# Chained down products, ScalarE evictions and VectorE products in a Hymba encoder layer

## The chip, the core and the metric

The kernel runs on one core of a Trainium2 chip. TensorE multiplies matrices into PSUM; VectorE, ScalarE and GpSimd (DVE, ACT and POOL in the rows) work element by element, the first two from PSUM or SBUF, and SyncE (SP) issues the DMAs. Each engine runs its own instructions strictly in its program order and waits at semaphores for the others. The metric is the device time of one execution in microseconds.

## What is computed

One bidirectional encoder layer for 1024 positions of width 1024, in float32. Cut to what matters here:

```python
h = modulate(rms_norm(x, attn_norm_w), sh_a, sc_a)
q_g, k_g, v_g, r_g, lr_f, lr_b, q_d, k_d, v_d = split_columns(h @ w_in, IN_SIZES)
o_a = gla_chunked(q, k, v, decay_fwd) + flipped gla_chunked(..., decay_bwd)   # 4 heads, chunks of 64
o_a = rms_norm(o_a, gla_norm_w) * silu(r_g)
a   = softmax(q1 k1 + bias) - lam * softmax(q2 k2 + bias)                    # 4 heads, blocks of 128 queries
o_b = rms_norm(a @ v_d, diff_norm_w) * (1 - lambda_init)
x   = x + g_a * (concat(o_a, o_b) @ w_out)
h2  = modulate(rms_norm(x, ffn_norm_w), sh_f, sc_f)
gate, val = split(depthwise_conv3(h2 @ w_up, conv_w, conv_b))
x   = x + g_f * ((silu(gate) * val) @ w_down)                                # 2816 x 1024
out = rms_norm(x, final_norm_w)
```

## The kernel before

Every large product is made of three matmuls: an operand is split into a high part (a cast to fp32r on ScalarE, line 370) and the rest (a subtraction, line 371), and `mm3` adds high by high, high by low and low by high (lines 565 to 567). Up and down projections go by a Strassen scheme, seven products of half size in place of eight.

The stages in order of time: the first projections (to about 350 us); attention in 32 steps of one head and 128 queries each, with GLA worked in between in the first 16 steps and the output projection (`gen_wout`) in the last 16; the transition (second norm, transposes, the operands of up); the up products; the down products; the rest of the last outputs. A framework orders each engine's instructions from a simulated timeline, so the order of instructions on an engine isn't that of the code.

**Attention.** `att_probs` makes scores (line 842), adds the bias and takes the maximum on VectorE (845) and the exponential on ScalarE (850); twice, for the two maps. `att_mix` combines them (858, 860). `att_T` transposes the result into two PSUM tiles of four blocks and copies the first to `aT` by ScalarE (871), the second by VectorE (873). `att_out` multiplies with v (888), scales into `on` (889) and, once for four query blocks, normalises: squares, Ln and Exp on ScalarE (895 to 897), the product `on` by rstd on GpSimd (898).

**GLA.** Per head `gd`, the queries times a decay, is made on GpSimd (1022); `kn` is a ScalarE copy of transposed keys (1029) for the state matmuls (1034). The output of each half is normalised (1088 to 1098), multiplied by the gate on GpSimd (1099), and split: `ohi` on ScalarE, the low part `go` on GpSimd.

**Output projection.** The list `wo` in `KN` says how many pieces of it each of the last 16 attention steps takes in.

**Down.** Seven products p1, p7, p6, p5, p4, p3, p2, each with 11 units of 128 rows of w_down, 4 blocks t of 128 positions and 3 matmuls: 132 matmuls of 128x512. A step is a pair of units; `down_load` loads blocks of weights (da) and of the gated activations (db) three steps ahead, `down_prep` makes sums and splits one step ahead: `dp_hi` and `whi_dp` on ScalarE, `db_p` and `wlo_dp` on VectorE. Products at even places write four one-bank tiles (tags mm and ao), those at odd places two tiles of two banks each (tag S); the pools have two tiles of each tag, which is all of PSUM. `down_out` takes a block of a product out of PSUM as soon as its last matmul is in, and adds it to the running sums; p5 and p4 gate their sums with g_f, add them to the residual x1b and multiply by the final norm's weight, all on GpSimd (lines 1538, 1539, 1565, 1571); p3 and p2 do the last of it on VectorE and ScalarE, and end each block of 128 positions with a norm (1580 to 1585) and its output DMA.

## Time and profile before

| | us |
|---|---|
| median of 3 runs | 1389.1 |
| lowest and highest | 1386.96, 1390.07 |
| the profiled execution | 1388.06 |
| its span, first to last instruction | 1386.4 |
| TensorE busy in the span | 1302.7 |
| VectorE, ScalarE, GpSimd busy | 978.6, 634.5, 389.0 |
| mean granted clock of TensorE, of 2.4 GHz | 0.974 |

Read it from the stage downwards: windows tell how busy each engine is in a stretch and what clock TensorE had; waits tell what ended the idle time of an engine; the timeline lists single instructions with their start and length. Busy time of matmuls overlaps a little, since one is 0.39 us long and the next starts 0.227 us later.

### The profile page before, as it was taken

The numbers are of one execution on the slowest core, as the hardware profiler recorded it, in microseconds if no ns is written. First come the engines' busy times: TensorE is split into PE (matmuls) and PEld (weight loads), VectorE is DVE, ScalarE is ACT, GpSimd is POOL, SyncE is SP. The second block draws the span as 40 slices with busy tenths as digits, with TensorE's granted clock in tenths as the row PEclk, the third lists the DMA queues.
The fourth block names the chain that finished last, engine by engine and source line by source line (L and its number), as shares of the span: only waits on it lengthen the run. The fifth ranks groups of instructions, "written<-read, shape, count | busy, mean of one in ns | idle before, by whom it ended". The sixth has DMA issues, their size and how long they took to land.

```text
span 1386.4 us, 17727 instructions
## 1 busy us (share of the span) xinstructions
PE 1302.7 (94%) x6244; PEld 1069.5 (77%) x6244; DVE 978.6 (71%) x1433; ACT 634.5 (46%) x1058; POOL 389.0 (28%) x284
## 2 busy tenths in 40 slices
...
GB/s 275 216 70 229 175 215 226 297 330 359 343 230 206 210 217 256 284 259 221 207 61 68 130 98 106 100 96 119 129 129 122 114 170 149 388 254 178 143 47 122
DMA packets 197873, 261.57 MB, mean 189 GB/s; under 512 B 13914, under 2 KB 122711, under 8 KB 197783
## 3 DMA queue, kind: packets, MB, share of 16 engines
...
## 4 chain that ended last, share of the span: by engine, by line
PE 69%; DVE 12%; DMA 5%; issue 4%; ACT 3%; POOL 3%; SPq 2%; ACTq 0%; DVEq 0%; POOLq 0%
PE st_up_b L565 4%; PE st_up_b L566 4%; PE st_up_b L567 4%; PE s L842 3%; PE dp L566 3%; PE dp L565 3%; PE dp L567 3%; PE o L888 3%; PE st_up_c L566 3%; PE st_up_c L567 3%; PE st_up_c L565 3%; PE st_up_a L566 2%; PE st_up_a L565 2%; PE st_up_a L567 2%; PE wo_ps L567 2%
## 5 line engine op out<-in xcount | busy, mean ns | idle before, releaser
L371 POOL TENSOR_TENSOR wlo_up<-raw_up,whi_up 128x512 fp32r<-128x512 f32 x132 | 176.3, 1342 | 211.7 <-ACT whi_up L370 203.5
L370 ACT CAST whi_up<-raw_up 128x512 fp32r<-128x512 f32 x132 | 80.8, 618 | 110.9 <-PE st_up_b L566 61.1
L566 PE MATMUL dp<-wlo_dp,dp_hi 128*128 128x512 f32 x308 | 121.1, 393 | 8.3 <-DVE wlo_dp L371 8.3
L565 PE MATMUL dp<-whi_dp,dp_hi 128*128 128x512 f32 x308 | 119.9, 391 | 2.8 <-DVE dacc L1562 2.8
L567 PE MATMUL dp<-whi_dp,db_p 128*128 128x512 f32 x308 | 119.0, 391 | 0.0
L566 PE MATMUL st_up_b<-t_lo,whi_up 128*128 128x512 f32 x264 | 103.4, 392 | 4.4 <-DVE t_lo L394 4.4
L565 PE MATMUL st_up_b<-t_hi,whi_up 128*128 128x512 f32 x264 | 103.6, 393 | 3.8 <-ACT t_hi L390 2.7
L567 PE MATMUL st_up_b<-t_hi,wlo_up 128*128 128x512 f32 x264 | 102.8, 390 | 0.0
L850 ACT ACTIVATE p<-p,mx 128x1024 f32<-128x1024 f32 x64 | 73.5, 1149 | 50.1 <-DVE mx L845 49.8
L845 DVE CUSTOM_DVE_ANT_0 p<-s,bias 128x1024 f32<-128x1024 f32 x64 | 77.3, 1217 | 14.9 <-PE s L842 12.9
L1432 ACT ACTIVATE cv<-u,cw 128x1024 f32<-128x1024 f32 x44 | 53.2, 1210 | 61.0 <-DVE u L433 61.0
L842 PE MATMUL s<-k,q 128*128 128x512 f32 x256 | 78.0, 427 | 2.4 <-DMA k<-k_d 1.5
L566 PEld LDWEIGHTS dp<-wlo_dp,dp_hi 128*128 128x128 f32 x308 | 58.1, 189 | 22.4 <-DVE wlo_dp L371 10.4
L371 DVE TENSOR_TENSOR wlo_dp<-da_p,whi_dp 128x512 fp32r<-128x512 f32 x77 | 67.8, 896 | 8.1 <-ACT whi_dp L370 7.9
L888 PEld LDWEIGHTS o<-vd,aT 128*128 128x128 f32 x512 | 66.7, 199 | 6.8 <-issue 1.7
L371 DVE TENSOR_TENSOR db_p<-db_p,dp_hi 128x1024 fp32r<-128x1024 f32 (+1 forms) x42 | 59.6, 1425 | 16.9 <-ACT dp_hi L370 16.9
L565 PE MATMUL st_up_a<-b_hi,whi_up 128*128 128x512 f32 x176 | 68.9, 392 | 2.3 <-DVE b L384 1.3
L565 PEld LDWEIGHTS dp<-whi_dp,dp_hi 128*128 128x128 f32 x308 | 58.2, 189 | 15.3 <-DVE dacc L1562 3.2
L888 PE MATMUL o<-vd,aT 128*128 128x128 f32 x512 | 68.8, 284 | 0.9 <-ACT aT L871 0.9
L370 ACT CAST whi_dp<-da_p 128x512 fp32r<-128x512 f32 x77 | 46.4, 620 | 49.5 <-PE dp L567 37.5
L566 PE MATMUL st_up_a<-b_lo,whi_up 128*128 128x512 f32 x176 | 68.5, 389 | 0.0
L567 PEld LDWEIGHTS dp<-whi_dp,db_p 128*128 128x128 f32 x308 | 58.3, 189 | 12.1
...
## 6 DMA issues: line engine op xcount, KB each, us to landing
...
```

What stands on the lines that cost most here:

```text
L370: S.copy(out=dst_hi, in_=src)
L371: lo_eng.tensor_tensor(out=dst_lo, in0=src, in1=dst_hi.bitcast(F32), op=ALU.subtract)
L565: T.matmul(ps, wh, rh, start=first, stop=False, skip_group_check=more)
L566: T.matmul(ps, wh, rl, start=False, stop=False, skip_group_check=more)
L567: T.matmul(ps, wl, rh, start=False, stop=last, skip_group_check=more)
L842: T.matmul(s[:, tsl(n)], q4[:, 2 * m + sw, :], kd[h][m][:, tsl(n)], start=(sw == 0), stop=(sw == 1))
L845: V.tensor_tensor_reduce(out=t, in0=s, in1=bias, scale=1.0, scalar=3.0e38, op0=ALU.add, op1=ALU.min, accum_out=mx)
L850: S.activation(t, t, AF.Exp, scale=-1.0, bias=mx, accum_out=z[:, m:m + 1])
L888: T.matmul(o_ps, aT[:, k, :], vd[h // 2][k // 4][:, k % 4, psl(h % 2)], start=(k == 0), stop=(k == KT - 1))
L1432: S.activation(t, u[b], AF.Identity, scale=cw[:, 44 + ci:45 + ci], bias=cw[:, 132 + ci:133 + ci])
```

## The change

Down's order becomes p1 p2 p6 p7 p5 p4 p3, and products that share outputs are accumulated on top of one another in PSUM: p2 on p1, p7 and then p4 on p6, p3 on p5. `down_out` so adds running sums less often: s1 is p1, s2 is p6 + p1 from PSUM, s3 is p7 (on p6) + p1, and p5 and p4 come on those. The block a12 is loaded twice, x1b's first half at the start of p2. The first four position blocks are finished in p4 (`finish`, with final weights), the others in p3.

In attention both halves of aT are copied by ScalarE; `gd`, the gate product with the low split behind it, and the product with rstd move from GpSimd to VectorE. The list `wo` is 2 2 and 3 3 where it was 1 1 and 2 4.

```diff
-  'wo': [3, 2, 2, 2, 2, 2, 1, 1, 2, 4, 3, 3, 3, 2, 3, 3], ... 'x01': (3, 4)
+  'wo': [3, 2, 2, 2, 2, 2, 2, 2, 2, 3, 3, 3, 3, 2, 3, 3], ... 'x01': (3, 3), ...
+  'dord': 'p1 p2 p6 p7 p5 p4 p3', 'aTs': '01', 'ons': 0, 'goe': 'VV', 'q3v': 1, 'onv': 1
...
-            if g == KN["aT"]:
+            if str(g) in KN["aTs"]:
                 S.copy(out=aT[:, 4 * g:4 * g + 4, :], in_=ps)
...
-        G.tensor_tensor(out=on, in0=on, in1=ss.unsqueeze(2).to_broadcast([P, 4, P]), op=ALU.mult)
+        if KN["onv"]:
+            V.tensor_tensor(out=on, in0=on, in1=ss.unsqueeze(2).to_broadcast([P, 4, P]), op=ALU.mult)
...
-        G.tensor_tensor(out=q3.rearrange("p (n c) -> p n c", c=CH), in0=q2.rearrange("p (n c) -> p n c", c=CH),
+        (V if KN["q3v"] else G).tensor_tensor(out=q3.rearrange("p (n c) -> p n c", c=CH), in0=q2.rearrange("p (n c) -> p n c", c=CH),
...
-            G.tensor_tensor(out=o, in0=o, in1=r_t[:, tsl(th)], op=ALU.mult)
+            eg[KN["goe"][0]].tensor_tensor(out=o, in0=o, in1=r_t[:, tsl(th)], op=ALU.mult)
...
-            split(hi, lo, o, G)
+            split(hi, lo, o, eg[KN["goe"][1]])
...
-    LOADS = {"p1": ("a11",), "p7": ("a21",), "p6": ("a22",), "p5": ("a21", "a22"), "p4": (), "p3": ("a12",), "p2": ()}
+    LOADS = {"p1": ("a11",), "p2": ("a12", "a21"), "p6": ("a22",), "p7": (), "p5": ("a21", "a22"), "p4": (), "p3": ("a12",)}
+    BANK = {"p1": ("A", True), "p2": ("A", False), "p6": ("B", True), "p7": ("B", False), "p4": ("B", False),
+            "p5": ("C", True), "p3": ("C", False)}
...
-            mm3(prods[p][t], bh[:, i, psl(t)], bl[:, i, psl(t)], *ws[i], u == 0, u == NU - 1)
+            mm3(ps_of[t], bh[:, i, psl(t)], bl[:, i, psl(t)], *ws[i], new and u == 0, u == NU - 1, not new)
...
+        elif p == "p2":
+            x1_add(t, 0, ps, half(f"dt_{p}{t}"), (V, G))
+            half_sq(t, 0)
+        elif p == "p6":
+            tmp = half(f"dt_{p}{t}", tag="sum")
+            V.tensor_tensor(out=tmp, in0=ps, in1=s1, op=ALU.add)
+            s2_of[t] = tmp
         elif p == "p7":
-            acc2[t] = half(f"dacc2_{t}")
-            S.copy(out=acc2[t], in_=ps)
+            V.tensor_tensor(out=kept(s3_of), in0=ps, in1=s1, op=ALU.add)
...
         elif p == "p5":
-            V.tensor_tensor(out=tmp, in0=ps, in1=acc2[t], op=ALU.add)
-            V.tensor_tensor(out=acc1[t], in0=ps, in1=acc1[t], op=ALU.add)
+            tmp = s3_of[t // 2][:, t % 2, :]
+            V.tensor_tensor(out=tmp, in0=ps, in1=tmp, op=ALU.add)
...
-            x1_add(4 + t, 0, acc1[t], acc1[t], (G, G))
+            x1_add(4 + t, 0, s2_of[t], s2_of[t], (G, G))
         elif p == "p4":
-            V.tensor_tensor(out=acc2[t], in0=ps, in1=acc2[t], op=ALU.add)
-            x1_add(t, 1, acc2[t], acc2[t], (G, G))
+            V.tensor_tensor(out=tmp, in0=ps, in1=s1, op=ALU.add)
+            x1_add(t, 1, tmp, tmp, (G, G))
             half_sq(t, 1)
-            G.tensor_tensor(out=x1[t][:, TH:], in0=x1[t][:, TH:], in1=fin_w[:, TH:], op=ALU.mult)
-            p1 = p1_of[t // 2][:, t % 2, :]
-            x1_add(t, 0, p1, p1, (G, G))
+            finish(t, False)
...
+        else:
+            V.scalar_tensor_tensor(out=o, in0=o, scalar=rs, in1=fin_w, op0=ALU.mult, op1=ALU.mult)
+            nc.sync.dma_start(out=out[0, psl(t), :], in_=o)
```

What this does to the order of instructions, at the places that the prediction speaks of. First ScalarE in the GLA half of attention, around the cast `ohi` of head 0 and the copy `kn2` of the keys of head 2, before:

```order
L850 ACTIVATE p1_3_1_4744,z_1_3_4711<-p1_3_1_4744,mx_1_3_1_4745 128x1024
L370 CAST ohi0_0_4558<-go0_0_4536 128x512
L1088 COPY go0_1_4638<-go0_1_4625 128x512
L850 ACTIVATE p2_0_0_4783,z_2_0_4786<-p2_0_0_4783,mx_2_0_0_4784 128x1024
L1090 ACTIVATE gsq0_1_4640<-go0_1_4638 128x512
L895 ACTIVATE osq_1_3_4886,oss_1_0_4591<-on1_0_4590 128x128
L1096 ACTIVATE gsq0_1_4640<-ms0_1_4642,eps_c_88 128x512
L1097 ACTIVATE gsq0_1_4640<-gsq0_1_4640 128x512
L370 CAST ohi0_1_4648<-go0_1_4638 128x512
L1029 COPY kn2_0_4793<-kn_ps2_0_4794 128x512
```
and after, from the same exponential on:

```order
L370 CAST ohi0_0_4558<-go0_0_4536 128x512
L1094 COPY go0_1_4638<-go0_1_4625 128x512
L1096 ACTIVATE gsq0_1_4640<-go0_1_4638 128x512
L871 COPY aT1_2_4753<-aT_ps1_2_0_4754 128x512
L871 COPY aT1_2_4753<-aT_ps1_2_1_4760 128x512
L850 ACTIVATE p1_3_1_4744,z_1_3_4711<-p1_3_1_4744,mx_1_3_1_4745 128x1024
L1102 ACTIVATE gsq0_1_4640<-ms0_1_4642,eps_c_88 128x512
L850 ACTIVATE p2_0_0_4783,z_2_0_4786<-p2_0_0_4783,mx_2_0_0_4784 128x1024
L1103 ACTIVATE gsq0_1_4640<-gsq0_1_4640 128x512
L898 ACTIVATE osq_1_3_4886,oss_1_0_4591<-on1_0_4590 128x128
L370 CAST ohi0_1_4648<-go0_1_4638 128x512
```
Between the two casts `ohi` the second copy of aT has come in; `kn2_0` follows the second `ohi` as before.

VectorE at the end of p5, whose evictions (`dt_p52`, `dacc1_2`) stand among splits for p4 and p3, before:

```order
L371 TENSOR_TENSOR wlo_dp4_3_0_12123<-da22_p5_3_11762,whi_dp4_3_0_12122 128x512
L1495 TENSOR_TENSOR da11_p1_2_10961<-da12_p3_2_12236,da11_p1_2_10961 128x1024
L371 TENSOR_TENSOR db_p3_0_12156<-db_p3_0_12156,dp3_hi0_12241 128x1024
L371 TENSOR_TENSOR wlo_dp4_3_1_12127<-da22_p5_3_11762,whi_dp4_3_1_12126 128x512
L1561 TENSOR_TENSOR dt_p52_12014<-dp5_1_11779,dacc2_2_11507 128x512
L1562 TENSOR_TENSOR dacc1_2_11751<-dp5_1_11779,dacc1_2_11751 128x512
L371 TENSOR_TENSOR wlo_dp4_4_0_12170<-da22_p5_4_11806,whi_dp4_4_0_12169 128x512
```
VectorE at the end of p6 after the change, where p6's sums (`dt_p60` and on) stand among splits for p7:

```order
L371 TENSOR_TENSOR wlo_dp7_1_1_11785<-da21_p2_1_11223,whi_dp7_1_1_11784 128x512
L1578 TENSOR_TENSOR dt_p60_11758<-dp6_0_11564,dp1_0_11279 128x512
L371 TENSOR_TENSOR db_p7_4_11812<-db_p7_4_11812,dp7_hi4_11900 128x1024
L371 TENSOR_TENSOR wlo_dp7_2_0_11818<-da21_p2_2_11260,whi_dp7_2_0_11817 128x512
L1578 TENSOR_TENSOR dt_p61_11763<-dp6_0_11564,dp1_0_11279 128x512
L1578 TENSOR_TENSOR dt_p62_11768<-dp6_1_11565,dp1_2_11288 128x512
L1578 TENSOR_TENSOR dt_p63_11773<-dp6_1_11565,dp1_2_11288 128x512
```
A split of 128x1024 and one of 128x512 lie between the first and the second eviction out of the tile `dp6_0`.

TensorE at the end of the first product in the tiles of two banks, p7 before:

```order
L567 MATMUL dp7_0_11296<-whi_dp7_5_0_11450,db_p7_5_11364 128x512
L565 MATMUL dp7_1_11297<-whi_dp7_5_0_11450,dp7_hi5_11447 128x512
L566 MATMUL dp7_1_11297<-wlo_dp7_5_0_11451,dp7_hi5_11447 128x512
L567 MATMUL dp7_1_11297<-whi_dp7_5_0_11450,db_p7_5_11364 128x512
L565 MATMUL dp6_0_11530<-whi_dp6_0_0_11486,dp6_hi0_11483 128x512
L566 MATMUL dp6_0_11530<-wlo_dp6_0_0_11487,dp6_hi0_11483 128x512
L567 MATMUL dp6_0_11530<-whi_dp6_0_0_11486,db_p6_0_11404 128x512
```
and p6 after, where the tile's second block and p7 follow:

```order
L565 MATMUL dp6_1_11565<-whi_dp6_5_0_11714,dp6_hi5_11711 128x512
L566 MATMUL dp6_1_11565<-wlo_dp6_5_0_11715,dp6_hi5_11711 128x512
L567 MATMUL dp6_1_11565<-whi_dp6_5_0_11714,db_p6_5_11632 128x512
L565 MATMUL dp6_0_11564<-whi_dp6_5_0_11714,dp6_hi5_11711 128x512
L566 MATMUL dp6_0_11564<-wlo_dp6_5_0_11715,dp6_hi5_11711 128x512
L567 MATMUL dp6_0_11564<-whi_dp6_5_0_11714,db_p6_5_11632 128x512
L565 MATMUL dp6_0_11564<-whi_dp7_0_0_11747,dp7_hi0_11744 128x512
L566 MATMUL dp6_0_11564<-wlo_dp7_0_0_11748,dp7_hi0_11744 128x512
L567 MATMUL dp6_0_11564<-whi_dp7_0_0_11747,db_p7_0_11670 128x512
```
Before, p6's matmuls into other tiles (`dp6_0_11530` and on) follow, and p7's last block comes 20 rows later; after, p6's block t=1 and then p7 itself go into `dp6_0` at once.

GpSimd around the products' sums of p5, before:

```order
L1539 TENSOR_TENSOR x1b_3_12164<-x1b_3_12164,dp1_2_11274 128x512
L1538 TENSOR_TENSOR dt_p50_11986<-dt_p50_11986,g_f_10712 128x512
L1538 TENSOR_TENSOR dacc1_0_11739<-dacc1_0_11739,g_f_10712 128x512
L1539 TENSOR_TENSOR x1b_4_11928<-x1b_4_11928,dt_p50_11986 128x512
L1539 TENSOR_TENSOR x1b_4_11928<-x1b_4_11928,dacc1_0_11739 128x512
L1565 TENSOR_TENSOR x1b_4_11928<-x1b_4_11928,fin_w_11970 128x512
L1538 TENSOR_TENSOR dt_p51_12000<-dt_p51_12000,g_f_10712 128x512
L1538 TENSOR_TENSOR dacc1_1_11745<-dacc1_1_11745,g_f_10712 128x512
L1539 TENSOR_TENSOR x1b_5_11930<-x1b_5_11930,dt_p51_12000 128x512
L1539 TENSOR_TENSOR x1b_5_11930<-x1b_5_11930,dacc1_1_11745 128x512
```
and after, from p6's sums on:

```order
L1556 TENSOR_TENSOR x1b_6_11896<-x1b_6_11896,dt_p62_11768 128x512
L1555 TENSOR_TENSOR dt_p63_11773<-dt_p63_11773,g_f_10712 128x512
L1556 TENSOR_TENSOR x1b_7_11898<-x1b_7_11898,dt_p63_11773 128x512
L1555 TENSOR_TENSOR dp7_0_11993<-dp7_0_11993,g_f_10712 128x512 x2
L1556 TENSOR_TENSOR x1b_4_11892<-x1b_4_11892,dp7_0_11993 128x512
L1555 TENSOR_TENSOR dp7_2_12002<-dp7_2_12002,g_f_10712 128x512
L1556 TENSOR_TENSOR x1b_5_11894<-x1b_5_11894,dp7_0_11993 128x512
L1555 TENSOR_TENSOR dp7_2_12002<-dp7_2_12002,g_f_10712 128x512
L1587 TENSOR_TENSOR x1b_4_11892<-x1b_4_11892,fin_w_12014 128x512
L1556 TENSOR_TENSOR x1b_6_11896<-x1b_6_11896,dp7_2_12002 128x512
L1587 TENSOR_TENSOR x1b_5_11894<-x1b_5_11894,fin_w_12014 128x512
L1556 TENSOR_TENSOR x1b_7_11898<-x1b_7_11898,dp7_2_12002 128x512
```
The sums of p6 (`dt_p60` to `dt_p63`) have come ahead of those of p5, and p1's are gone.

## Rows read from the trace of the kernel before

**Rows 1.** Windows by stage: attention with GLA and output projection, the down products, and the rest after the last matmul. Columns: length, busy time (and instructions) of each engine, TensorE's granted clock, the DMA engines' busy share and rate.

```profile
350.00:700.00 350.00, 328.87 (x2006) 280.99 (x2005) 237.63 (x433) 174.28 (x359) 50.36 (x41) 0.96 0.78 237
...
1153.97:1378.08 224.11, 213.01 (x925) 173.95 (x923) 179.55 (x190) 100.87 (x169) 79.52 (x44) 0.99 0.52 184
1378.08:1386.40 8.32, 0.00 (x1) 0.00 (x0) 3.21 (x7) 3.83 (x11) 0.00 (x0) 0.82 0.54 203
```
**Rows 2.** The same view, the down stage cut by product (132 matmuls each): p1, p7, p4, p3, p2.

```profile
1153.97:1183.89 29.92, 29.92 (x133) 24.78 (x132) 24.93 (x30) 13.72 (x18) 0.00 (x0) 1.00 0.53 195
1183.89:1213.81 29.92, 29.92 (x133) 24.78 (x132) 27.44 (x32) 20.23 (x29) 0.00 (x0) 1.00 1.05 387
...
1273.65:1306.67 33.02, 30.23 (x133) 24.70 (x132) 30.66 (x24) 12.73 (x23) 31.79 (x19) 1.00 0.46 154
1306.67:1348.00 41.33, 33.02 (x133) 25.53 (x132) 38.29 (x33) 16.33 (x30) 30.51 (x17) 0.96 0.17 57
1348.00:1378.08 30.08, 30.08 (x133) 24.59 (x131) 16.37 (x31) 14.04 (x36) 0.00 (x0) 1.00 0.21 84
```
**Rows 3.** Timeline of TensorE in p4 at its one long wait: the instruction that had waited, with start and length in us; in brackets the idle time before the instruction and what ended it.

```profile
1292.92 0.50 PE L565 MATMUL dp<-whi_dp,dp_hi 128*128 128x512 f32 x1 [2.79 <-DVE dacc L1562]
```
**Rows 4.** Timeline of VectorE in the same stretch of p4:

```profile
1286.54 1.23 DVE L1495 TENSOR_TENSOR da_p<-da_p,da_p 128x1024 f32<-128x1024 f32 x1 [2.31 <-DMA da_p<-in_w_down_dram]
1287.68 2.31 DVE L371 TENSOR_TENSOR db_p<-db_p,dp_hi 128x1024 fp32r<-128x1024 f32 x1
1289.92 1.75 DVE L371 TENSOR_TENSOR wlo_dp<-da_p,whi_dp 128x512 fp32r<-128x512 f32 x1
1291.59 0.68 DVE L1561 TENSOR_TENSOR dt_p<-dp,dacc 128x512 f32<-128x512 f32 x1
```

and of the stretch around 1242 us:

```profile
1242.50 0.68 DVE L371 TENSOR_TENSOR wlo_dp<-da_p,whi_dp 128x512 fp32r<-128x512 f32 x1
```
**Rows 5.** Timeline of TensorE in p3, the instructions that had waited over 0.5 us.

```profile
1309.50 0.50 PE L566 MATMUL dp<-wlo_dp,dp_hi 128*128 128x512 f32 x1 [2.44 <-DVE wlo_dp L371]
...
1313.42 0.50 PE L566 MATMUL dp<-wlo_dp,dp_hi 128*128 128x512 f32 x1 [0.90 <-DVE wlo_dp L371]
...
1328.02 0.50 PE L566 MATMUL dp<-wlo_dp,dp_hi 128*128 128x512 f32 x1 [0.70 <-DVE wlo_dp L371]
...
1333.17 0.50 PE L566 MATMUL dp<-wlo_dp,dp_hi 128*128 128x512 f32 x1 [2.14 <-DVE wlo_dp L371]
...
1341.04 0.50 PE L566 MATMUL dp<-wlo_dp,dp_hi 128*128 128x512 f32 x1 [2.13 <-DVE wlo_dp L371]
```
**Rows 6.** TensorE's waits in attention, 350 to 700 us: who waited for whom, total us, times, the longest.

```profile
PE u_ps L1034 <- ACT kn L1029: 8.2, 2, 4.3
PE aT_ps L869 <- DVE p L860: 2.3, 3, 1.6
PE aT_ps L869 <- DVE on L889: 2.3, 1, 2.3
...
PE o L888 <- ACT aT L871: 0.9, 2, 0.7
```
**Rows 7.** Groups of instructions by line and shape, 345 to 700 us: count, busy us, mean ns of one, idle time of the engine before them and what ended it.

```profile
L850 ACT ACTIVATE p<-p,mx 128x1024 f32<-128x1024 f32 x64 | 73.5, 1149 | 50.1 <-DVE mx L845 49.8
...
L860 DVE SCALAR_TENSOR_TENSOR p<-p,rb,p 128x1024 f32<-128x1024 f32 x32 | 41.0, 1283 | 0.8
...
L873 DVE COPY aT<-aT_ps 128x512 f32<-128x512 f32 x32 | 22.0, 687 | 7.9 <-PE aT_ps L869 7.7
...
L871 ACT COPY aT<-aT_ps 128x512 f32<-128x512 f32 x32 | 18.6, 583 | 19.9 <-PE aT_ps L869 19.7
...
L371 POOL TENSOR_TENSOR go<-go,ohi 128x512 fp32r<-128x512 f32 x8 | 10.7, 1339 | 6.0 <-ACT ohi L370 5.3 <-DVE mx L845 0.7
...
L1099 POOL TENSOR_TENSOR go<-go,gr 128x512 f32<-128x512 f32 x8 | 10.2, 1276 | 62.0 <-DVE go L1098 56.6 <-PE aT_ps L869 5.4
...
L898 POOL TENSOR_TENSOR on<-on,oss 128x512 f32<-128x512 f32 x8 | 9.9, 1236 | 180.7 <-ACT oss L897 144.3 <-DVE mx L845 36.3
...
L1022 POOL TENSOR_TENSOR gd<-gq,dc_sh 128x1024 f32<-128x1024 f32 x4 | 7.6, 1906 | 36.5 <-DMA k_d<-qk_hi 21.9 <-DMA gq<-g_d 14.6
```
**Rows 8.** Timelines at the two waits for kn: ScalarE and GpSimd at 426 us, and GpSimd at 462 us.

```profile
429.84 0.62 ACT L370 CAST ohi<-go 128x512 fp32r<-128x512 f32 x1 [2.17 <-POOL go L1099]
430.36 0.58 ACT L1029 COPY kn<-kn_ps 128x512 f32<-128x512 f32 x1
...
428.54 1.27 POOL L1099 TENSOR_TENSOR go<-go,gr 128x512 f32<-128x512 f32 x1 [5.16 <-DVE go L1098]
...
462.21 1.91 POOL L1022 TENSOR_TENSOR gd<-gq,dc_sh 128x1024 f32<-128x1024 f32 x1
466.08 1.26 POOL L1099 TENSOR_TENSOR go<-go,gr 128x512 f32<-128x512 f32 x1 [1.97 <-DVE go L1098]
```
**Rows 9.** Groups of instructions by line and shape in the down stage, columns as in rows 7.

```profile
L1545 ACT ACTIVATE acc_sq<-x1b 128x512 bf16<-128x512 f32 x16 | 10.0, 626 | 36.4 <-POOL x1b L1539 22.3 <-DVE x1b L1539 14.1
...
L1581 ACT ACTIVATE ors<-ors,eps_c 128x1 f32<-128x1 f32 x8 | 2.4, 294 | 1.7 <-DVE ors L1580 1.7
...
L1551 ACT COPY dp<-dp 128x512 f32<-128x512 f32 x4 | 2.2, 596 | 0.0
L1582 ACT ACTIVATE ors<-ors 128x1 f32<-128x1 f32 x8 | 1.5, 200 | 0.2
```

More of the change, by code (lines that the diff above doesn't have):

```diff
@@ L1492, in down_prep, with sums @@
         at = lambda b: blks[(b, q)][:, 0:n, :]
-        if p in SUMS:
-            o, i0, i1, op = SUMS[p]
-            V.tensor_tensor(out=at(o), in0=at(i0), in1=at(i1), op=ALU.add if op == "+" else ALU.subtract)
+        def sums(of):
+            for o, i0, i1, op in of.get(p, ()):
+                V.tensor_tensor(out=at(o), in0=at(i0), in1=at(i1), op=ALU.add if op == "+" else ALU.subtract)
+        sums(SUMS)
         a, b = OPS[p]
@@ L1503, in down_prep @@
             ws.append((hi, lo))
+        sums(AFTER)
         ops_of[s] = (ws, bh, bl)
@@ L1507, in down_mms @@
         p, q = steps[s]
-        if q == 0:
-            if ORDER.index(p) % 2 == 1:
+        bank, new = BANK[p]
+        if q == 0 and new:
+            if bank == "B":
                 two = [s_ps(f"d{p}_{i}") for i in range(2)]
-                prods[p] = [two[t // 2][:, tsl(t % 2)] for t in range(4)]
+                banks[bank] = [two[t // 2][:, tsl(t % 2)] for t in range(4)]
             else:
-                prods[p] = [mm_ps(f"d{p}_{t}", tag=("mm", "ao")[t // 2]) for t in range(4)]
+                banks[bank] = [mm_ps(f"d{p}_{t}", tag=("mm", "ao")[t // 2]) for t in range(4)]
+        ps_of = banks[bank]
         todo = [s] + list(t_outer)
```

74 lines of the change are left out of this document (39 added, 35 removed).

## Prediction

> **What bounds the kernel now.** I read the stages first, by windows [rows 1]. From 1153.97 to 1378.08 us, the seven down products, TensorE is busy 213.0 of 224.1 us; attention with GLA, 350 to 700, has it busy 328.9 of 350 at a granted clock of 0.96 of 2.4 GHz. TensorE is the engine that matters in both, so the questions are where it stands still and which engine ends each wait. Cutting the down stage by product [rows 2] shows that p1, p7 and p2 run at 29.92 to 30.08 us for 132 matmuls, 0.227 us each. Seven products at 29.92 are 209.4, so 14.7 us are lost, nearly all in two: p4 takes 33.02 (3.1 over) and p3 41.33 (11.4 over). In just these two GpSimd is busy 31.8 and 30.5 us, with 36 of the stage's 44 large operations, and VectorE 30.7 and 38.3. In p1, p7 and p2 GpSimd does nothing.
>
> The waits say the same. In p4 TensorE stops for 2.79 us until dacc, line 1562, has left a pair of banks [rows 3]. VectorE had that eviction behind two splits of 2.31 and 1.75 us; beside an idle GpSimd the same 128x512 split took 0.68 [rows 4]. So a GpSimd operation beside a VectorE operation with two SBUF operands costs VectorE some 1.07 us, while the evictions, with one operand in PSUM, stayed at 0.68. In p3 five waits on wlo_dp add to 8.31 us [rows 5], and the window's clock is 0.96, so part of the remainder of 11.4 is time at the lower level (1.2 GHz) after them.
>
> In attention the longest kind is TensorE's wait for kn, 8.2 us in two waits [rows 6]. The place at 426 us [rows 8]: kn's copy on ScalarE stands in program order behind the cast ohi, which waits 2.17 us for the gate product on GpSimd (1.27 us).
>
> **Down, what goes.** Chaining takes eight of GpSimd's operations out of the stage's end: 44 become 32, and of these only p5's 12 and p4's 8 fall beside p4 and p3, 20 in place of 36. The order bears this out: p6's eight (dt_p60 to dt_p63) now stand ahead of p5's. At 1.07 us, 16 fewer give VectorE 17 us; p5 evicts once, not twice (4 fewer at 0.68, 2.7 us), and p4's finish adds four 128x1024 operations at some 1.28 (line 860's, rows 7), 5.1. VectorE's 69.0 us in the two windows [rows 2] become 69.0 - 17.1 - 2.7 + 5.1 = 54.3, against 59.8 of pure matmul time. Before, 69.0 and the waits between filled 74.4; now 5 us are spare. I count the whole 14.7 us as removed, and then charge what is late next.
>
> **Down, what comes.** (a) p6 to p7. In the order, VectorE has dt_p60, then db_p7_4 and wlo_dp7_2_0, then dt_p61; TensorE has p6's block t=1 waiting for dt_p60 (they share a tile of two banks, as in rows 3) and p7's first matmul, into that tile, waiting for dt_p61. Before, p6's matmuls into other banks stood there. From the end of dt_p60: 128x1024 split some 1.23 (as a 128x1024 sum that issued ahead of GpSimd; 2.31 for a split behind it, rows 4), split 0.68, eviction 0.68, make 2.6 us, of which block t=1's three matmuls cover 0.7; the first wait adds 0.4. That is 2.3 us, and 3.4 if dt_p60's own product on GpSimd falls beside the splits; I take 2.8. (b) p1 to p2, four separate banks, four ScalarE copies at 0.60 [rows 9]: six matmuls (1.36 us) stand between the last one into a bank and p2's first into it, so 0 to 0.8; I take 0.2. (c) p2's loads: three 512 KB blocks a step and the 2 MB of x1b at its beginning, where p7 before had two a step and the DMA engines were full (1.05 of their time, 387 GB/s, rows 2) without a stall: 0 to 1.5, I take 0.5. p3 has one more reload of a12, at a share of 0.17, hidden. (d) p4's finish inside p3. VectorE has x1b_0's final product ahead of dt_p41, dt_p42 and the next weight splits, and it waits for a chain: two GpSimd operations (1.27 alone, about 2 beside VectorE), a square of 0.63, two small activations of 0.29 and 0.20 [rows 8, 9]. With eviction, splits and hand-overs this is 9 to 10.5 us after p4's end. p4's last block, which needs dt_p42, stands 53 matmuls (12.0 us) after it, so the margin is about 2 us. But GpSimd's twelve p5 operations at 2 us end only 24 to 27 us into p4's 30; should it be late by 4 us, TensorE waits 2 and the splits behind lose as much: 0 to 4, I take 1.5. p6, p7, p5 and p4 evict on VectorE where p7 had copies on ScalarE: 0.68 each in windows with VectorE at 20 to 27 of 30 us, covered. The tail after the last matmul, 8.3 us [rows 1], is the same code on the last product and stays.
>
> Sum for down: 2.8 + 0.2 + 0.5 + 1.5 = 5.0 us of new waits, so 14.7 - 5.0 = 9.7 us gained; between the ends, 5 to 12.
>
> A rule speaks against (a) and (b). The rows show what a shared tile costs, 2.79 us in one place [rows 3]. The Trainium skill, Perfetto Trace Analysis, section Matmuls, says that independent groups of matmuls should rotate through different PSUM banks, so that the eviction of one overlaps the next. By it each hand-over into the same banks is exposed; p4 and p3 come a whole product later and escape it. What that would give is the third case below.
>
> **Attention.** The 32 second halves of aT go from VectorE (0.687 each, 22.0 us) to ScalarE (0.583, 18.7 us more, on 174 busy of 350) [rows 1, 7]. VectorE takes 28 operations that GpSimd has: gate 8, split 8, rstd 8 at 128x512, some 0.69 each alone, and four 128x1024 at some 1.2, together 21.4; its load is thus even. What changes is the length of chains. Gate product: 1.27 us and a hand-over become 0.69 on the engine that has just written its operand, with the output cast sooner. At the other wait for kn, near 464, GpSimd had gd (1.91 us) ahead of the gate product as well [rows 8]. I take 2.5 of the 8.2 us as gained, 0 to 5. On the other side VectorE now holds the lo split right behind the product, and so stands while ScalarE makes ohi (0.61 us, eight times): at most 5 us of VectorE, whose share is 68%, hidden. The output projection's table gives two matmul groups to steps that had one and three to one that had four: 0 to 3, I take 1.5. The second aT copy comes straight behind the first on ScalarE, so the second half is 0.58 us later than in parallel; TensorE's waits for VectorE's p and on (2.3 us each) fall a little as VectorE's copies go, and its o matmuls have work ahead of them for most steps (waits for aT of 0.9 us in all, rows 6). I take the copies at nothing on balance, bounds -3 to +18.7. Sum: 4.0 us gained.
>
> On contention the rows show little here: the two-operand line 860 takes 1.283 us on average beside attention's GpSimd work, where the 128x1024 sum that issued ahead of GpSimd took 1.23 in down [rows 4, 7], so at most 32 x 0.05 = 1.7 us return. The Trainium skill, SBUF — State Buffer, section Who interferes with whom, says that a VectorE instruction with two SBUF inputs contends with GpSimd's reads and that the second to issue blocks fully; had all 28 operations met one, some 30 us of VectorE would come back. The rows put it at a twentieth of that, and I do not count it.
>
> **Rivals.** 1, the forecast: both parts pay, 1389.1 - 9.7 - 4.0 = 1375.4 us. I count against the median, 1.0 above the profiled run's 1388.06, because the 14.7 us lie in the program's order and would be in every run. Chance 0.45.
> 2. Down pays, attention comes out even: ScalarE gets its copies late by as much as kn comes sooner. For: TensorE's recorded waits in attention are scattered, and most are ended by several engines. 1379.4. Chance 0.2.
> 3. The hand-overs eat down's gain. The order puts p7's first matmul behind two evictions with two splits between; with both hand-overs exposed for four evictions and two contended splits (2.7 + 1.9, twice, 9.2 us) and attention at -2: about 1387. Against: p2's bank order leaves six matmuls of cover. Chance 0.1.
> 4. Attention returns more: its clock is 0.96 of 350 us, 14 us; were half of that to come back with the kn waits, 15 us in place of 4.0: 1364.4. Chance 0.12.
> 5. Slower: ScalarE becomes attention's bound. In program order the second copy of aT waits behind an exponential of 1.149 us (line 850) which itself waits for VectorE's maximum; with the o matmuls of each of 32 steps exposed to its 0.58 us, 18.7 us are lost: 1389.1 - 9.7 + 18.7 = 1398.1. It is slower than before from 0.3 us per step on (9.7 / 32). For: 50.1 us of ScalarE's idle time stand ahead of line 850, waiting on VectorE [rows 7]; against: ScalarE stays at 55%. Chance 0.13.
>
> **How the numbers follow.** The likeliest is 1375.4. From 1364 to 1388 I leave out case 5 and a little of case 4's lower end, 2 in 10. A measurement of this kernel tells some 0.2% (2.8 us) from no change. Faster: cases 1, 2, 4 and part of 3, 0.81; within: 0.06; slower: case 5, 0.13.
>
> **What would show it.** Down: p4 and p3 at 30 to 32 us each with GpSimd near 24 and 16; one TensorE wait of 2 to 3.5 us at the head of p7 ended by line 1578; short splits beside the first three products. Attention: waits for kn under 6 us in total, line 871 at 64 copies, and waits of TensorE on aT that stay under 3 us; case 5 would show them at over 10. I am wrong if p3 still shows waits on wlo_dp that add to over 5 us, or if TensorE's clock in attention falls.

## The result

| | median us | runs | ratio to the kernel before, 95% interval |
|---|---|---|---|
| kernel before, beside it | 1390.07 | 9 | |
| the change | 1381.05 | 9 | 0.9936 [0.9914, 0.9957] |

The change is faster by 9.0 us (by the interval 6 to 12), where 13.7 were forecast; the profiled execution has a span of 1377.6 us at a granted clock of 0.975, 8.8 less than before. Single runs of either kernel lie up to 6 or 8 us from their median, so a part worth a few microseconds is read better from a stage of the trace than from whole runs.

The profile after, by windows as in [rows 1, 2]: attention from its first score matmul to the first matmul of up, then the seven products p1, p2, p6, p7, p5, p4, p3, and the rest.

```profile
359.80:703.60 343.80, 323.17 (x2001) 275.47 (x2000) 236.08 (x432) 193.73 (x398) 15.58 (x15) 0.98 0.77 237
1153.26:1183.18 29.92, 29.92 (x133) 24.78 (x132) 21.95 (x26) 13.73 (x19) 0.00 (x0) 1.00 0.57 206
1183.18:1214.03 30.85, 30.08 (x133) 24.59 (x132) 24.92 (x30) 16.68 (x24) 0.00 (x0) 1.00 1.05 387
1214.03:1243.95 29.92, 29.81 (x131) 24.06 (x129) 25.75 (x29) 16.28 (x27) 8.40 (x5) 1.00 0.69 240
1243.95:1276.57 32.62, 30.09 (x134) 24.93 (x134) 16.46 (x21) 9.37 (x14) 11.20 (x8) 1.00 0.58 194
1276.57:1306.49 29.92, 29.92 (x134) 24.77 (x133) 22.00 (x28) 14.12 (x19) 0.24 (x1) 1.00 0.48 145
1306.49:1337.26 30.77, 30.09 (x132) 24.32 (x131) 30.65 (x24) 15.75 (x27) 22.34 (x12) 1.00 0.53 183
1337.26:1368.50 31.24, 31.21 (x137) 25.26 (x135) 24.39 (x34) 10.87 (x32) 13.49 (x8) 1.00 0.19 75
1368.50:1377.60 9.10, 0.00 (x0) 0.00 (x0) 3.72 (x7) 4.33 (x11) 0.00 (x0) 0.64 0.55 206
```

From the first down matmul to the last it is 215.2 us where it was 224.1. The windows are cut by time, so they don't hold the same number of matmuls: p6's has three loads of weights fewer than p1's (129 against 132) and hides a short stop in its 29.92, and p3's has three more (135). p1 and p5 run at their 29.92 with nothing lost. p4, 33.02 before, is at 30.77, and the last two windows together are 2.2 us over the floor of 59.84, 0.7 to 0.9 of it for the matmuls that the last has more, where p4 and p3 were 14.5 over [rows 2]. GpSimd still works 22.3 us in p4 but 13.5 in p3, and VectorE, 38.3 us in p3 before, is at 24.4; its 69.0 us in the two windows became 55.0. The rest after the last matmul is 9.1 us, 0.8 longer than before [rows 1].

TensorE's waits in the down stage after:

```profile
PE dp L565 <- DVE dt_p L1578: 2.5, 1, 2.5
PE dp L565 <- ACT dp_hi L370: 0.8, 1, 0.8
PE dp L566 <- DVE wlo_dp L371: 0.7, 1, 0.7
```

The largest new one, with the instruction that had waited and VectorE in front of it (start, length; in brackets the idle time before and what ended it):

```profile
1242.51 0.39 PE L567 MATMUL dp<-whi_dp,db_p 128*128 128x512 f32 x1
...
1246.50 0.47 PE L565 MATMUL dp<-whi_dp,dp_hi 128*128 128x512 f32 x1 [2.53 <-DVE dt_p L1578]
...
1247.26 0.40 PE L565 MATMUL dp<-whi_dp,dp_hi 128*128 128x512 f32 x1
```

```profile
1242.26 0.69 DVE L1578 TENSOR_TENSOR dt_p<-dp,dp 128x512 f32<-128x512 f32 x1 [2.05 <-PE dp L567]
1242.87 1.22 DVE L371 TENSOR_TENSOR db_p<-db_p,dp_hi 128x1024 fp32r<-128x1024 f32 x1
1244.00 1.75 DVE L371 TENSOR_TENSOR wlo_dp<-da_p,whi_dp 128x512 fp32r<-128x512 f32 x1
1245.67 1.27 DVE L1578 TENSOR_TENSOR dt_p<-dp,dp 128x512 f32<-128x512 f32 x2
```

It is the place of the prediction's (a): dt_p60, the 1.22 us split, a second split that GpSimd stretches from 0.68 to 1.75 us, and only then dt_p61, for which p7's first matmul waits. It was taken at 2.8. The long wait is 2.5 us, but the place costs more: from the matmul at 1242.51 to the one at 1247.26, seven later, 4.75 us pass where seven take 1.59. So 3.2 us are lost, 0.4 of them at the first stop, for dt_p60, and the rest at the second.

The splits of the stage, groups by line and shape, show the rest of the load coming off: wlo_dp falls from 907 to 830 ns on average and db_p from 1502 to 1302, over the same 73 and 34 instructions.

```profile
L371 DVE TENSOR_TENSOR wlo_dp<-da_p,whi_dp 128x512 fp32r<-128x512 f32 x73 | 59.1, 830 | 20.2 <-ACT whi_dp L370 20.0
...
L371 DVE TENSOR_TENSOR db_p<-db_p,dp_hi 128x1024 fp32r<-128x1024 f32 x34 | 44.1, 1302 | 9.5 <-ACT dp_hi L370 8.7 <-DMA da_p<-in_w_down_dram 0.9
```

In attention the waits of TensorE over 1 us now read:

```profile
PE u_ps L1040 <- ACT kn L1035: 5.1, 2, 3.6
PE h_ps L380 <- DVE x L1337: 3.1, 1, 3.1
PE s L842 <- DMA k<-k_d: 2.6, 2, 2.0
PE aT_ps L869 <- DVE p L860: 1.8, 1, 1.8
PE o L888 <- ACT aT L871: 1.2, 1, 1.2
...
PE kn_ps L1034 <- ACT gs L1047: 1.1, 2, 0.6
```

kn's waits fell from 8.2 to 5.1 us, and the wait for on from 2.3 us to 0.2. But h_ps, the transposes for the second norm, waits 3.1 us (1.3 before) and the scores 2.6 us for keys that a DMA brings (1.5 before). The same stretch of the kernel before, by its window:

```profile
355.40:704.30 348.90, 327.77 (x2001) 279.99 (x2000) 240.07 (x436) 176.62 (x366) 51.99 (x42) 0.96 0.77 234
```

The stage is 5.1 us shorter in this execution, 343.8 for 348.9. But TensorE stands still in it for 20.6 us where it stood still for 21.1 (length less busy time). The other 4.6 us are the same matmuls taking less time, 323.2 us for 327.8, at a granted clock of 0.98 for 0.96. And the first projections, which no edit reaches, took 4.4 us more here: the first score matmul comes at 359.8 us and came at 355.4. So the profiled spans differ by -5.1 + 4.4 - 8.9 (down) + 0.8 (the rest) = -8.8 us.

The groups by line and shape of the moved work:

```profile
L850 ACT ACTIVATE p<-p,mx 128x1024 f32<-128x1024 f32 x64 | 73.6, 1152 | 25.4 <-DVE mx L845 24.6 <-DVE rz L856 0.5
...
L871 ACT COPY aT<-aT_ps 128x512 f32<-128x512 f32 x64 | 35.7, 585 | 39.5 <-PE aT_ps L869 39.3
...
L1106 DVE TENSOR_TENSOR go<-go,gr 128x512 f32<-128x512 f32 x8 | 5.5, 690 | 0.1
L371 DVE TENSOR_TENSOR go<-go,ohi 128x512 fp32r<-128x512 f32 x8 | 5.5, 688 | 2.7 <-ACT ohi L370 2.7
L902 DVE TENSOR_TENSOR on<-on,oss 128x512 f32<-128x512 f32 x8 | 5.5, 688 | 2.1 <-ACT oss L900 2.1
...
L1028 DVE TENSOR_TENSOR gd<-gq,dc_sh 128x1024 f32<-128x1024 f32 x4 | 4.9, 1220 | 0.0
```

The copies on ScalarE are twice as many at the same length, and the products on VectorE take 0.69 and 1.22 us, as estimated, with nothing of the length that they had on GpSimd [rows 7].

### The profile page after: what moved, and what is told of

Read it like the earlier page. It is cut to its first block, busy times and chain, and to the rows that moved or that the text cites. A ratio compares the mean times of both kernels' runs of the same rounds, so it can differ in the third digit from the quotient of the medians.

```text
span 1377.6 us, 17662 instructions
## 1 busy us (share of the span) xinstructions
PE 1300.0 (94%) x6244; PEld 1066.3 (77%) x6244; DVE 962.7 (70%) x1425; ACT 647.9 (47%) x1082; POOL 324.9 (24%) x244
## 4 chain that ended last, share of the span: by engine, by line
PE 71%; DMA 10%; DVE 10%; issue 3%; ACT 2%; SPq 1%; POOL 1%; ACTq 0%; DVEq 0%; POOLq 0%
PE st_up_b L565 4%; PE st_up_b L566 4%; PE st_up_b L567 4%; PE s L842 3%; PE dp L565 3%; PE dp L566 3%; PE dp L567 3%; PE o L888 3%; PE st_up_c L566 3%; PE st_up_c L567 3%; PE st_up_c L565 3%; PE st_up_a L567 2%; PE st_up_a L565 2%; PE st_up_a L566 2%; PE pr_qk L565 2%
## 5 line engine op out<-in xcount | busy, mean ns | idle before, releaser
L567 PE MATMUL dp<-whi_dp,db_p 128*128 128x512 f32 x308 | 115.6, 389 | 0.0
L842 PE MATMUL s<-k,q 128*128 128x512 f32 x256 | 75.1, 418 | 4.2 <-DMA k<-k_d 2.6
L371 DVE TENSOR_TENSOR wlo_dp<-da_p,whi_dp 128x512 fp32r<-128x512 f32 x77 | 61.7, 824 | 20.2 <-ACT whi_dp L370 20.0
L567 PE MATMUL st_up_a<-b_hi,wlo_up 128*128 128x512 f32 x176 | 68.0, 392 | 0.0
```

Source lines behind the costliest of these rows:

```text
L371: lo_eng.tensor_tensor(out=dst_lo, in0=src, in1=dst_hi.bitcast(F32), op=ALU.subtract)
L567: T.matmul(ps, wl, rh, start=False, stop=last, skip_group_check=more)
L842: T.matmul(s[:, tsl(n)], q4[:, 2 * m + sw, :], kd[h][m][:, tsl(n)], start=(sw == 0), stop=(sw == 1))
```

## The experiments

In all, a stage is measured in the one profiled execution of the run, and a time is the median with its ratio to the kernel before on the same chip.

**e1_down: down's part alone.** The change with the keys of attention set back.

```diff
-  'wo': [3, 2, 2, 2, 2, 2, 2, 2, 2, 3, 3, 3, 3, 2, 3, 3], ... 'aTs': '01', ... 'goe': 'VV', 'q3v': 1, 'onv': 1
+  'wo': [3, 2, 2, 2, 2, 2, 1, 1, 2, 4, 3, 3, 3, 2, 3, 3], ... 'aTs': '0', ... 'goe': 'GG', 'q3v': 0, 'onv': 0
```

> Down's part alone (attention, GLA and the output projection as before). Theory: two thirds of the gain are down's, 14.7 us of waits less some 5 us of new ones, and 1 us more after the last matmul: first down matmul to the last about 215 us where it was 224.1, the stretch from attention's first score matmul to the first matmul of up unchanged at 365 us; 1380 to 1383 beside a kernel before of 1390. Rival, down pays nothing over a whole run since its gain comes back as longer waits at the end: within 3 us of the kernel before.

1383.3 us, ratio 0.9963 [0.9941, 0.9985], down 215.7 us, attention 365.4 us on the measure of the expectation (to the first st_up_b matmul). Down alone makes the kernel faster, by 5.1 us (2 to 8), where 7 to 10 were expected. In the trace its stage saves about what it saves in the full change, and the wait for dt_p is there again with 2.5 us.

**e2_att: attention's part alone.** The kernel before with the other edits, down untouched.

```diff
-            if g == KN["aT"]:
+            if str(g) in KN["aTs"]:
...
-        G.tensor_tensor(out=on, in0=on, in1=ss.unsqueeze(2).to_broadcast([P, 4, P]), op=ALU.mult)
+        if KN["onv"]:
+            V.tensor_tensor(out=on, in0=on, in1=ss.unsqueeze(2).to_broadcast([P, 4, P]), op=ALU.mult)
...
```

> Attention's part alone (list wo, both aT copies on ScalarE, gd, gate, low split and rstd product on VectorE), down as before. Theory: 4 us, by shorter chains to kn and a more even output projection: first score matmul to the first matmul of up 361 us where it was 365, down's matmuls 224 us; 1386 beside 1390. Rival (attention even): 365 and no difference. Rival (ScalarE's copies are the bound): 370 and more, with waits of TensorE for aT of over 10 us in all.

1386.9 us, ratio 0.9987 [0.9964, 1.001]: not to be told from no change over whole runs, and not from the 4 us of the theory either. The stage took 359.2 us on the same measure (364.9 in the kernel before), kn's waits 5.1, and TensorE waited for aT 1.4 us: rival 5's sign is absent. What the stage's length is worth, e8 and e9 tell. Down, which this run doesn't touch, took 222.3 us where the kernel before took 224.1, with waits of the same size (8.3 and 2.6) but at a granted clock of 1.00 for 0.99; so the 8.9 us that the change saves there hold a share of up to 2 us that differs between executions.

**e3_between and e8_between_again: a product of other banks between every two that are chained.**

```diff
-  'dord': 'p1 p2 p6 p7 p5 p4 p3'
+  'dord': 'p1 p6 p2 p7 p5 p4 p3'
...
-    LOADS = {"p1": ("a11",), "p2": ("a12", "a21"), "p6": ("a22",), ...
+    LOADS = {"p1": ("a11",), "p2": ("a12",), "p6": ("a21", "a22"), ...
...
-    AFTER = {"p2": (("a21", "a11", "a21", "-"),)}
-    SUMS = {"p6": (("a11", "a22", "a21", "-"),), ...
+    AFTER = {}
+    SUMS = {"p6": (("a21", "a11", "a21", "-"), ("a11", "a22", "a21", "-")), ...
...
-        if s == X0:
+        if s == NQD + X0:
```

> The change with down's order p1 p6 p2 p7 p5 p4 p3: a product in other banks stands between every two that are chained, so the next one into the same banks never follows its eviction at once. a21 is loaded for p6 in place of p2, x1b's first half six steps later. Theory: the wait of 2.5 us for dt_p at p6 to p7 is a price of the chain in the same tile and goes; the late dp_hi in the second product (0.9 us) stays or moves to p6, whose step now has the three loads: down's matmuls 212 us where they are 215. Rival: the wait is VectorE's load at that place, not the shared tile; then a wait of about the same size appears at another product.

1377.4 us, ratio 0.9911 [0.988, 0.9941], down 211.0. The down stage and the rest by windows, and TensorE's only wait in it:

```profile
1153.10:1364.10 211.00, 210.32 (x925) 172.98 (x923) 168.66 (x186) 96.78 (x161) 56.52 (x32) 1.00 0.59 208
1364.10:1373.20 9.10, 0.00 (x0) 0.00 (x0) 3.73 (x7) 4.34 (x11) 0.00 (x0) 0.62 0.55 207
```

```profile
PE dp L566 <- DVE wlo_dp L371: 0.7, 1, 0.7
```

The 2.5 us wait is gone, and none took its place, neither here nor in any other run with this order: the chain into the same tile is what exposed it, not VectorE's load. The late dp_hi of the second product (0.8 us) has gone as well; whether by the later load of x1b or by the new order of the weights' loads, these runs don't tell. 211.0 is 1.6 over seven times 29.92.

> The interleaved version again, unchanged, beside the three others on their chip. Down's matmuls should take 211 us again. If attention's stage length is set by the clock that the execution is granted, it lies anywhere from 343 to 348 us with the same recorded waits, and follows the granted clock of its first half; if it is set by the waits alone, it comes out within 1 us of 348.2.

1377.25 us, ratio 0.9914 [0.9882, 0.9945], down 211.0 again. Attention had the same order of instructions in both, but took 348.1 us in e3_between and 345.7 here, while kn's waits were 5.1 in both. So the stage's length moves by 2.4 us with one order, and with the clock: 0.96 in e3_between (0.94 in its first 175 us), and 0.98 here, in its first 175 us too:

```profile
356.30:702.00 345.70, 322.62 (x2001) 275.00 (x2000) 235.14 (x432) 193.99 (x398) 15.59 (x15) 0.98 0.78 237
```

**e4_noweight: GpSimd's weight products left out of the kernel before.**

```diff
-            G.tensor_tensor(out=x1[4 + t][:, TH:], in0=x1[4 + t][:, TH:], in1=fin_w[:, TH:], op=ALU.mult)
...
-            G.tensor_tensor(out=x1[t][:, TH:], in0=x1[t][:, TH:], in1=fin_w[:, TH:], op=ALU.mult)
```

> The kernel before without its eight GpSimd products by the final norm's weight (lines 1565 and 1571), which leaves the second halves of the output without that weight; 28 of the 36 GpSimd operations stay in p4 and p3. Theory (GpSimd beside VectorE's two-operand splits is what makes p4 and p3 late): 8 x 1.07 = 8.6 us of VectorE come back, and p4 and p3 together fall from 74.4 to 64 to 69 us. Rival (shared bank pairs and the order of evictions are what makes them late): p4 and p3 stay within 2 us of 74.4.

It ran once. p4 and p3 by windows, and TensorE's waits in the stage:

```profile
1276.28:1309.90 33.62, 30.09 (x122) 24.35 (x121) 31.02 (x25) 13.33 (x24) 29.42 (x18) 0.90 0.46 155
1309.90:1343.20 33.30, 32.80 (x145) 26.86 (x144) 29.97 (x32) 16.18 (x30) 16.96 (x9) 1.00 0.20 71
```

```profile
PE dp L565 <- DVE dacc L1562: 3.5, 1, 3.5
PE dp L566 <- DVE wlo_dp L371: 0.5, 1, 0.5
```

p4 and p3 take 33.62 + 33.30 = 66.9 us where they took 74.4. All of it comes from p3, which is 8.0 us shorter: waits on wlo_dp of 8.31 us [rows 5] are down to 0.5. p4's wait for dacc in the bank pair, 2.79 before, is still there at 3.53, with a granted clock of 0.90 in p4's window, where it was 1.00. So the theory holds for p3 and the rival for p4's one wait: less GpSimd work doesn't help an eviction that stands in VectorE's order behind a weight sum and two splits, while that sum waits for its load (2.36 us in this run, 2.31 before [rows 4]).

**e5_copy_back, e6_pool_back, e7_wo_back: attention's three parts taken back one at a time,** on the interleaved version.

```diff
-  'aTs': '01'
+  'aTs': '0'
```

> The interleaved version (p1 p6 p2 p7 p5 p4 p3) with the second aT copy back on VectorE. Theory of the prediction: the copies come out at nothing, so waits of TensorE for kn stay at 5.1 us, and the attention stage (first score matmul to first matmul of up) at 343 to 348 us. Rival: VectorE freed of 22 us of copies is what lets VectorE take the products, so kn's waits go back to 7 us or more. Rival: ScalarE's copies cost, and the stage is shorter by over 5 us.

1381.6 us, ratio 0.9942 [0.9918, 0.9967]; stage 347.6, kn's waits 6.2, down 210.9. The waits for kn lie between the theory's 5.1 and the rival's 7.

```diff
-  'goe': 'VV', 'q3v': 1, 'onv': 1
+  'goe': 'GG', 'q3v': 0, 'onv': 0
```

> The interleaved version with gd, gate product, low split and rstd product back on GpSimd, both aT copies on ScalarE. Theory: these products are what shortened the chain to kn, so its waits go back from 5.1 to about 8.2 us, and the stage grows by 2 to 4 us. Rival: the gain in attention comes from elsewhere (the copies, the list wo, or the clock), and the waits for kn stay near 5.1.

1384.0 us, ratio 0.9953 [0.993, 0.9976]; kn's waits 6.8, again between the two, so copies and products both had a part in the 5.1. In the profiled execution, the longest of its 12 at 1391.8 us, the stage took 362.7 us at a clock of 0.94, its slowest anywhere, and the waits grew in many places:

```profile
357.90:720.60 362.70, 333.87 (x2002) 283.29 (x2002) 217.03 (x404) 194.29 (x398) 53.43 (x42) 0.94 0.74 223
```

```profile
PE u_ps L1040 <- ACT kn L1035: 6.8, 2, 4.3
PE h_ps L380 <- DVE x L1337: 4.4, 1, 4.4
PE s L842 <- DMA k<-k_d: 3.4, 3, 2.7
```

```diff
-  'wo': [3, 2, 2, 2, 2, 2, 2, 2, 2, 3, 3, 3, 3, 2, 3, 3]
+  'wo': [3, 2, 2, 2, 2, 2, 1, 1, 2, 4, 3, 3, 3, 2, 3, 3]
```

> The interleaved version with the old list wo (1 1 and 2 4 in place of 2 2 and 3 3). Theory: 1.5 us lost, in waits between 590 and 640 us. Rival: no difference, since the work of the output projection is the same and only moves; recorded waits of the stage within 1 us of the interleaved version's.

1374.9 us, ratio 0.9902 [0.9871, 0.9933]: not slower, and 2.4 us under the interleaved version by the medians. Repeated:

> The interleaved version with the old list wo, a second time. If the old list is no worse than the new one: 1374 to 1377.5, at or under the interleaved version's 1377.3. If the first time was chance and the new list pays 1.5 us: 1378 to 1380.

1374.7 us, ratio 0.9886 [0.9859, 0.9913]. Both times the old list was the quicker; the intervals overlap, so I say that the even spread pays nothing, and may cost some 2 us. The wait of h_ps is 1.5 and 1.6 us with the old list, and 3.1, 2.1 and 2.2 with the new one in the change and the two interleaved runs.

**e9_between_old_att: the interleaved order with attention as before.**

> The interleaved down order with attention, GLA and the list wo as in the kernel before. Down should take 211 us again. Theory: attention's parts are worth 2 to 4 us together, while each of the two (copies, products) alone is worth nothing or a loss, since each lifts the load of the engine that the other would fill; so about 1380 to 1381, waits for kn 8.2, stage 348 to 351. Rival (the parts add up, 4 us for the copies and 6 for the products): 1386 and more.

1376.9 us, ratio 0.9904 [0.9877, 0.9932], less than the theory and the rival expect; kn's waits 8.2 again, down 211.2, and the stage, by its window,

```profile
362.30:707.40 345.10, 324.22 (x2001) 278.06 (x2000) 240.12 (x436) 176.61 (x366) 51.98 (x42) 0.97 0.77 235
```

345.1 us, shorter than the interleaved runs with the new attention, 348.1 and 345.7. The parts do not add up: by the medians, products alone (e5) and copies alone (e6) are 4 and 7 us worse than both (the intervals touch), and both together, with either list, are within 2.2 us of neither.

**e11_finish_off: p4's final products off VectorE,** on the interleaved version with the old list.

```diff
-            V.scalar_tensor_tensor(out=o, in0=o, scalar=rs, in1=fin_w, op0=ALU.mult, op1=ALU.mult)
+            S.activation(o, o, AF.Copy, scale=rs)
+            G.tensor_tensor(out=o, in0=o, in1=fin_w, op=ALU.mult)
```

> As the last, with p4's final products off VectorE: the scaling by the row's factor on ScalarE, the weight product of 128x1024 on GpSimd. Theory: VectorE's in-order waits for p4's norm chain hold p3's last splits and the first block of the tail; without them the 0.85 us wait on wlo_dp in p3 goes and the stretch after the last matmul is 8.2 us again in place of about 9: 1 to 1.7 us less than the run beside it. Rival: the four products of 128x1024 on GpSimd beside the last splits make these late, and p3 has waits on wlo_dp of 2 us and more.

1374.9 us, ratio 0.9897 [0.9868, 0.9926], no gain. The windows of down and of the rest, and the group of the four products on GpSimd:

```profile
1149.80:1360.60 210.80, 210.12 (x925) 173.00 (x923) 166.76 (x179) 100.32 (x161) 66.24 (x36) 1.00 0.59 206
1360.60:1370.70 10.10, 0.00 (x0) 0.00 (x0) 5.04 (x10) 5.37 (x15) 0.00 (x0) 0.70 0.62 234
```

```profile
L1616 POOL TENSOR_TENSOR x1b<-x1b,fin_w 128x1024 f32<-128x1024 f32 x4 | 10.0, 2522 | 1.0 <-ACT x1b L1615 1.0
```

The wait on wlo_dp is still there, 0.7 us, so it isn't the norm chain that holds it, and the rest after the last matmul is 10.1 us, longer and not shorter. VectorE's timeline at the last product tells why. Each of its four blocks starts there with dt_p, the block out of PSUM times g_f. The first and the fourth, before:

```profile
1372.07 0.69 DVE L1538 TENSOR_TENSOR dt_p<-dp,g_f 128x512 f32<-128x512 f32 x1 [8.26 <-PE dp L567]
...
1378.19 0.68 DVE L1538 TENSOR_TENSOR dt_p<-dp,g_f 128x512 f32<-128x512 f32 x1
```

in the change, with p4's last final product (line 1615) ahead of the first:

```profile
1362.16 1.29 DVE L1615 SCALAR_TENSOR_TENSOR x1b<-x1b,ors,fin_w 128x1024 f32<-128x1024 f32 x1 [0.67 <-ACT ors L1606]
1363.36 0.69 DVE L1555 TENSOR_TENSOR dt_p<-dp,g_f 128x512 f32<-128x512 f32 x1
...
1369.12 0.69 DVE L1555 TENSOR_TENSOR dt_p<-dp,g_f 128x512 f32<-128x512 f32 x1
```

and in this run, where the first comes at 1354.58:

```profile
1355.31 1.57 DVE L1556 TENSOR_TENSOR x1b<-x1b,dt_p 128x512 f32<-128x512 f32 x1
...
1357.67 1.49 DVE L1604 TENSOR_TENSOR ors<-fss 128x1 f32<-128x1 f32 x1 [0.19 <-ACT acc_sq L1562]
...
1362.55 0.69 DVE L1555 TENSOR_TENSOR dt_p<-dp,g_f 128x512 f32<-128x512 f32 x1
```

The last matmul ends at 1378.08 before, at 1368.47 in the change and at 1360.60 here. Before, VectorE takes the first block as soon as its matmuls are done, 6.0 us ahead of that end. In the change it takes it 5.1 us ahead, 0.9 late, because the final product, itself waiting for the row factor (ors) from ScalarE, stands before it. VectorE needs 2.1 us for a block and TensorE brings one every 2.0, so the delay shrinks only to 0.5: the fourth block comes 0.65 us after the last matmul and not 0.11. In e11 the first block is on time again, 6.0 us ahead, but now two operations behind it run beside GpSimd's products: the sum takes 1.57 us where it took 0.69, the small sum for the row factor 1.49 where it took 0.16, and the fourth block comes 1.95 us after the last matmul. So the theory's cause of the longer rest was there, and the edit put a larger one in its place.

## Why the prediction was right, and where its sizes were off

The likeliest case held in direction and in the larger part of its size: 9.0 us of 13.7. What held is down's part; the step that failed is attention's 4.0 us.

**Down, what goes.** "I count the whole 14.7 us as removed": right. After, p4 and p3 have one wait on a split, of 0.7 us, and no time at the lower clock, and VectorE's 54.3 us in the two windows came out at 55.0. The cause, GpSimd beside VectorE's two-operand splits, is shown for p3 by e4, where eight GpSimd operations fewer gave back 7.4 us against 8.6 worked out. For the wait in p4's window the count of GpSimd operations was not the cause. It is a wait for p5's pair of banks, out of which dacc is taken, behind the work ahead of that eviction on VectorE; after the change p5 writes one-bank tiles, and no such wait is left at its end. That the tiles are the reason is argued from the code and not tested by itself.

**Down, what comes.** (a) 2.8 taken, 3.2 measured, at the place and by the instructions named, and shown by e3 to be the chain's price; it is nearer to the upper value, 3.4, since one of the two splits did run beside dt_p60's product on GpSimd. This price is what the rule on rotating independent groups of matmuls through banks (the Trainium skill, Perfetto Trace Analysis, section Matmuls) speaks of: by the runs it holds for the shared tiles of two banks at p6 to p7, a wait of 2.5 us, and not at p1 to p2, where six matmuls stand between and no wait is seen. (b) 0.2 taken, no wait seen. (c) 0.5 taken, 0.8 for dp_hi, whose cast had waited 1.5 us for a DMA. (d) 1.5 taken: the finish in p3 cost nothing on TensorE in the stage; a wait of 0.7 us on wlo_dp at the end of p4 is what there is. e11 shows that the norm chain isn't its cause; VectorE is busy 30.65 of p4's 30.77 us there beside GpSimd's 22.3, which speaks for what is left of the old contention. Sum 5.0 taken; 224.1 - 215.2 = 8.9 saved in the stage where 9.7 were forecast.

**The term that was missed** is the end. "The tail after the last matmul, 8.3 us, is the same code on the last product and stays": it grew to 9.1 in this execution and to 8.7 to 9.1 in every kernel with the new down stage and p4's finish on VectorE, while e2 and e4, with the old one, kept 8.2. The code is the same, but VectorE comes to it late. The chain of p4's finish, which (d) priced for the splits of p3 alone, holds the first block by 0.9 us, and the last element-wise operation ends 0.45 us later behind the last matmul than before (4.98 and 4.53). That is about half of the growth. The other half lies between that operation and the end of the output's DMA, 4.2 us in the change and 3.7 before; it is 3.75 to 4.16 in the kernels with the new down stage and 3.62 to 3.74 in those with the old one, and its cause stays open. So 8.9 - 0.8 = 8.1 us of 9.7 are left.

**Attention** is the step that failed: "Sum: 4.0 us gained". The mechanism read from the rows is there: kn's waits fall from 8.2 to 5.1 us in every kernel that has copies and products together, 3.1 where 2.5 were taken. With the wait for on, 5.2 us went; but the waits for the second norm's input, for keys not yet loaded and of kn_ps for a copy grew by 1.8, 1.1 and 1.1, and with smaller ones TensorE stands still for 20.6 us in the stage where it stood still for 21.1. The sum took each wait that goes as time gained and set nothing against it. "The output projection's table ... I take 1.5" had the wrong sign if any. The 1.7 us of contention that "at most" could return didn't: line 860 takes 1284 ns after and took 1283 before, when few of its 32 operations met one on GpSimd at all.

Over whole runs e2 shows 0.9987 [0.9964, 1.001], from 5.0 us gained to 1.4 lost. The change beside e1 (0.9936 and 0.9963) would put attention's edits at 3.8 us, and e9 beside e3 and e8 (0.9904, and 0.9911 and 0.9914) at nothing; the intervals overlap in both. So rival 2, "down pays, attention comes out even", describes what happened better than the forecast: its ratio of 1379.4 to 1389.1, 0.9930, lies within the measured interval, and the forecast's, 0.9901, just outside. What stays open is whether attention's edits are worth some 4 us or none.

Rival 3's mechanism (hand-overs) was there at a third of its price, 3.2 us of 9.2, since one hand-over waits, not both and four evictions. Rival 5 did not come: TensorE's waits for aT are 1.2 to 2.2 us in all kernels with the copies on ScalarE. Rival 4's way, the clock coming back, is hinted at and not shown: in the first 175 us of the stage the granted clock was 0.92 to 0.95 in four executions with the old attention and 0.94 to 0.98 in four with the new one. The 5.1 us by which the stage is shorter in the profiled execution are nearly all clock, so that they come near the forecast is no evidence for its mechanism.

By their ratios the two versions that the experiments point to come out ahead of the change (0.9936), though most of the intervals touch: the interleaved order (0.9911 and 0.9914), and that with the old list (0.9902 and 0.9886, 1374.7 and 1374.9 us).
